# Two chained sequence blocks: casts of square sums to another engine, one recurrence to another engine, and four numbers of the schedule

## Chip, cores and metric

The kernel runs on one core of one Trainium2 chip. The metric is device time in microseconds; three runs of a kernel are summed up by their median. One more execution is profiled, and everything read from a trace below comes from that one.

## What is computed

The input is a sequence of 2048 tokens of width 1024. Two blocks follow each other.

```python
# first block: state-space mixer and short convolution
proj = rmsnorm(x) @ w_in                 # u_ssm, z_ssm, h, b, c, z (512 wide each)
s[t] = ab * s[t-1] + bb * u_ssm[t]       # complex state, 32 groups of 64 states
y = gelu(Re(c . s) + d * u_ssm)
y_ssm = y * sigmoid(y @ w_glu + b_glu) * silu(z_ssm)
y_conv = b * conv3(c * h) * silu(z)
x = rmsnorm(x + [y_ssm, y_conv] @ w_out)
# second block: conv module, gated recurrence, chunked attention, FFN
sh1, sc1, g1, sh2, sc2, g2 = silu(c_2) @ w_ada + b_ada     # modulation rows
p = (x * (1 + sc1) + sh1) @ w_in_2
y = [conv_module(p), hgrn2(p), chunk_attention(p)] @ w_out_2
x = layer_norm(ALPHA * x + (1 + g1) * y)
h = x * (1 + sc2) + sh2
x = layer_norm(ALPHA * x + (1 + g2) * ((silu(h @ W_gate) * (h @ W_up)) @ w_ffn_out))
```

## The kernel before

Every large product is made of three float16 matmuls per block (`mm3`, L417 to L419): each operand is cut into a high and a low float16 half (`split`: the high half on ScalarE, L405, the low half on VectorE, L406). The cut needs a power-of-two scale of the whole tensor, which comes from its sum of squares: ScalarE squares and adds along the free axis (`sumsq`, L410), giving one float32 number for each of 128 partitions; `part` casts these to bfloat16 (L365, or L367 where two columns are added on the way), and `total` adds over the partitions with one matmul against a matrix of ones (L373); VectorE then makes the scale from the exponent (`pow2`, L354 to L356). So a cut waits for a load, then ScalarE, the cast, TensorE, VectorE, and then the two halves of the cut. Since TensorE works in the order in which its instructions stand, a `total` whose cast is late holds up all matmuls behind it.

`Weight` and `Loader` do this for weights in three steps (load, `stat`, `split`), with `d1` and `d2` as the distances between the steps counted in weights. `Pair` and `Feed` are the same for the FFN's input weights (`load`, `scale`, `cut`, numbered 0, 1, 2); `prime` runs the first `PRIME_N` of a list of such steps in the last stage before the FFN, and `FIRST` says which are run within the FFN's first products.

The order of the program is that of a list: the stages are Python loops over column blocks and blocks of 512 tokens, and `bg.tick()` in these loops advances background generators by a rate for each. The state-space work (`ssm_all`, four feature blocks `ssm_fb`), the modulation rows (`mod_rows`, twelve rows, L768 to L777) and the loads are such generators. A scheduler then puts the instructions of each engine into their order, so a small edit shifts orders far away from it.

Within `ssm_fb`, two chains of eight complex products (`cmul`, six element-wise instructions each of 128x64) make the matrices E and H. Both run on GpSimd (`gtt`, L360). H is copied into a zero-filled matrix by ScalarE (L647, L648); L821 is ScalarE's copy of a finished projection out of PSUM.

The stage after that (`stage_glu_mix`) projects z (L1002, SiLU), applies GELU to the recurrence's output (L945), multiplies by w_glu (sigmoid, L967), and multiplies by w_out for 16 tiles of 128 tokens (L1079 adds a half tile, L1048 scales a tile, L406 cuts it). Meanwhile `ConvAtt.prep` takes nine of the second block's weights through a `Loader`.

Of the kernel before, what the change touches and what calls it, by code (L numbers as in the profile page):

```python
# [11 lines left out]
BF16 = mybir.dt.bfloat16  # L12
# [3 lines left out]
ALU = mybir.AluOpType  # L16
AX = mybir.AxisListType
# [135 lines left out]
class Weight:  # L153
# [17 lines left out]
    def stat(self):  # L171
        k = self.k
        nc = k.nc
        n = len(self.raw)
        self.pair = k.pair([P, self.nkb, self.ncol], "w")
        ss = k.tiny("wss", n)
        for c, raw in enumerate(self.raw):
            if self.colmul is not None:
                cm = self.colmul[:, c * P:(c + 1) * P].unsqueeze(1).to_broadcast([P, self.nkb, P])
                k.gtt(raw, raw, cm, ALU.mult)  # L180
            if self.rowmul is not None:
                self.mul(raw, raw, self.rowmul.unsqueeze(2).to_broadcast([P, self.nkb, P]), ALU.mult)
            k.sumsq(self.pair[1][:, :, c * P:(c + 1) * P].bitcast(BF16), raw, out=ss[:, c:c + 1])
        if n > 1:
            t = k.tiny("wst")
            nc.vector.tensor_reduce(t, ss, axis=AX.X, op=ALU.add)
            ss = t
        self.cols = k.cols3.pop(0) if len(k.cols3) > 8 else k.hold(3)
        self.tot, self.s, self.inv = (self.cols[:, i:i + 1] for i in range(3))
        self.x = k.part(self.tot, ss)  # L190

    def split(self):
        k = self.k
# [77 lines left out]
class Kit:  # L271
# [87 lines left out]
    def gtt(self, out, x, y, op):  # L359
        self.nc.gpsimd.tensor_tensor(out, x, y, op)  # L360

    def part(self, col, a, b=None):
        x = col.bitcast(BF16)[:, :1]
        if b is None:
            self.nc.vector.tensor_copy(x, a)  # L365
        else:
            self.nc.vector.tensor_tensor(x, a, b, ALU.add)  # L367
        return x

    def total(self, x, out, tot=None):  # L370
        nc = self.nc
        ps = self.bank()
        nc.tensor.matmul(ps[:, :1], self.ones, x, start=True, stop=True)  # L373
        sq = ps[:, :1]
        if tot is not None:
            nc.vector.tensor_copy(tot, sq)
            sq = tot
        self.pow2(sq, out=out)
        self.unbank(ps)
# [174 lines left out]
def ssm_fb(k, a, pm, fb, u_d, y_d):  # L554
    nc = k.nc
    gp = nc.gpsimd
    v = nc.vector
    NP = 4
    prs = slice(fb * 4, fb * 4 + 4)
    shp = [P, NP, 16]  # L560
# [17 lines left out]
    Hr, Hi = new([P, NP, 8, 16], "Hr"), new([P, NP, 8, 16], "Hi")  # L578
    t1, t2 = new(shp, "cm1"), new(shp, "cm2")

    def cmul(orr, oi, xr, xi, yr, yi):
        k.gtt(t1, xi, yi, ALU.mult)
        k.gtt(orr, xr, yr, ALU.mult)
        k.gtt(orr, orr, t1, ALU.subtract)
        k.gtt(t2, xi, yr, ALU.mult)
        k.gtt(oi, xr, yi, ALU.mult)
        k.gtt(oi, oi, t2, ALU.add)

    cmul(Er[:, :, 0], Ei[:, :, 0], br, bi, bc("qr"), bc("qi"))
    k.free(br, bi)  # L590
    for j in range(7):
        cmul(Er[:, :, j + 1], Ei[:, :, j + 1], Er[:, :, j], Ei[:, :, j], bc("abr"), bc("abi"))
        if j == 3:
            yield
    yield
    C = []
    Cb = []
    for nm, c2 in zip(("ssm_c_re", "ssm_c_im"), cs2):
# [13 lines left out]
        C.append(c)  # L612
        Cb.append(cb)
    yield
    cmul(Hr[:, :, 0], Hi[:, :, 0], C[0], C[1], bc("abr"), bc("abi"))
    k.free(*C)
    for j in range(7):
        cmul(Hr[:, :, j + 1], Hi[:, :, j + 1], Hr[:, :, j], Hi[:, :, j], bc("abr"), bc("abi"))
        if j == 3:
            yield  # L620
    k.free(t1, t2)
# [159 lines left out]
def stage_in(k, a, dr):  # L781
# [95 lines left out]
    cw = k.new([P, 4, 3], F32, "cw")  # L877
    for j in range(3):
        nc.sync.dma_start(cw[:, :, j], a["conv_w"][0, j].rearrange("(f p) -> p f", p=P))
    mod = k.bg.add(mod_rows(k, a, dr["mod"]), 0.8)  # L880
    cols = [c + fb * P for fb in range(4) for c in (2048, 1024, 1536, 2560)] + [512 + f * P for f in range(4)]
    chunks = Loader([Weight(k, win[:, c:c + P], inv_x, rowmul=gain) for c in cols])
    at = 0
# [39 lines left out]
def stage_glu_mix(k, a, xT, chunks, ssm, mod, dr, nxt):  # L923
# [50 lines left out]
    def mp1(tb):  # L974
        cv = k.new([P, 4, TB], F32, "cv")
        nc.sync.dma_start(cv, dr["yv"][:, tb * TB:(tb + 1) * TB].rearrange("(k p) t -> p k t", p=P))
        gy = G[tb][0]
        pr = k.pair([P, KB, TB], "mp")
        s2 = k.tiny("ms", 2)
        k.sumsq(pr[1][:, 0:4].bitcast(BF16), gy, out=s2[:, 0:1])  # L980
        k.sumsq(pr[1][:, 4:8].bitcast(BF16), cv, out=s2[:, 1:2])
        s, inv = k.hold(), k.hold()
        k.part(inv, s2[:, 0:1], s2[:, 1:2])
        M[tb] = [gy, cv, pr, s, inv]

    def mp2(tb):
        gy, cv, pr, s, inv = M[tb]
        k.total(inv.bitcast(BF16)[:, :1], (s, inv))
        k.split(pr[0][:, 0:4], pr[1][:, 0:4], gy, s)
        k.split(pr[0][:, 4:8], pr[1][:, 4:8], cv, s)  # L990
        k.free(gy, cv)
        sc = k.hold(2)
        for n in range(2):
            v.tensor_tensor(sc[:, n:n + 1], inv, wo[n].get(0).inv, ALU.mult)
        M[tb] = (pr, sc)
# [150 lines left out]
class ConvAtt:  # L1146
# [8 lines left out]
    def prep(self, inv_h, hb2):  # L1155
        k, a = self.k, self.a
        nc, v = k.nc, k.nc.vector
        W2 = a["w_in_2"][0]
        W = lambda c0, n=P: Weight(k, W2[:, c0:c0 + n], inv_h, bound=c0 >= 2560)
        self.ws = Loader([W(256), W(384), W(0), W(128), W(2560), W(2816), W(2688), W(2944), W(3072, 256)])  # L1160
        yield from self.ws.run()
        w = self.ws.ws
        self.wg, self.wv, self.wq, self.wk, self.wvv = w[0:2], w[2:4], w[4:8:2], w[5:8:2], w[8]

        def bscale(w):
            q = k.tiny("bq")
            v.tensor_tensor(q, w.tot, hb2, ALU.mult)
            s, i = k.pow2(q, keep=True)
            e = k.hold()
            v.tensor_tensor(e, s, w.inv, ALU.mult)  # L1170
            return s, i, e

        self.sq = [bscale(x) for x in self.wq]
        self.sk = [bscale(x) for x in self.wk]
        self.sv = bscale(self.wvv)
        qks = []
        self.qki = []
        for f in range(2):
            t = k.hold()
            v.tensor_tensor(t, self.sq[f][0], self.sk[f][0], ALU.mult)  # L1180
            qks.append(t)
            t = k.hold()
            v.tensor_tensor(t, self.sq[f][1], self.sk[f][1], ALU.mult)
            v.tensor_scalar(t, t, 0.125, None, op0=ALU.mult)
            self.qki.append(t)
        yield
        self.B = yield from att_bias(k, a, self.dr["ext"], qks)
        self.cw = k.new([P, 2, self.KC], F32, "cw")
        self.cb = k.hold(2)
        for f in range(2):  # L1190
# [686 lines left out]
class Pair:  # L1877
# [8 lines left out]

    def scale(self):
        k = self.k
        ss = k.tiny("wss", 3)
        junk = k.new([P, 4, 2 * P], BF16, "junk")  # L1890
        for i in range(2):
            k.sumsq(junk, self.raw[i], out=ss[:, i:i + 1])
        k.free(junk)
        self.inv = k.hold()
        self.x = k.part(self.inv, ss[:, 0:1], ss[:, 1:2])

    def cut(self):
        k = self.k
# [377 lines left out]
EARLY_RATE = 0  # L2276
AHEAD = 1
PRIME_AT = 11
PRIME_N = 8
SSM_RATE = 1.0  # L2280


@with_exitstack
# [71 lines left out]
```

## Time and profile before

| | us |
|---|---|
| median of three runs (lowest, highest) | 3271.31 (3270.45, 3274.15) |
| profiled execution, its own time | 3276.22 |
| its span, first to last instruction | 3274.5 |
| TensorE busy | 3048.2 |
| VectorE busy | 2061.5 |
| ScalarE busy | 1116.8 |
| GpSimd busy | 760.0 |

Of the profiled execution's time, 1.7 us lie outside the span, and it is 4.9 us above the median of the three runs. TensorE is idle for 226.3 us of the span (3274.5 - 3048.2). The granted TensorE clock, averaged over the span, is 0.967 of full speed.

### The profile page before, as it was taken

The numbers are of one execution on the slowest core, as the hardware profiler recorded it, in microseconds if no ns is written. First come the engines' busy times: TensorE is split into PE (matmuls) and PEld (weight loads), VectorE is DVE, ScalarE is ACT, GpSimd is POOL, SyncE is SP. The second block draws the span as 40 slices with busy tenths as digits, with TensorE's granted clock in tenths as the row PEclk, the third lists the DMA queues.
The fourth block names the chain that finished last, engine by engine and source line by source line (L and its number), as shares of the span: only waits on it lengthen the run. The fifth ranks groups of instructions, "written<-read, shape, count | busy, mean of one in ns | idle before, by whom it ended". The sixth has DMA issues, their size and how long they took to land. (4 is left out here: it accounts for less than half of the span.)

```text
span 3274.5 us, 43302 instructions
## 1 busy us (share of the span) xinstructions
PE 3048.2 (93%) x16198; PEld 1532.2 (47%) x16198; DVE 2061.5 (63%) x4895; ACT 1116.8 (34%) x1745; POOL 760.0 (23%) x801
## 2 busy tenths in 40 slices
PE   6799999979799988999999878999999999899998
PEld 4344454534345654555555433444444444344443
DVE  5577887355864469999568877555555555543322
ACT  5322222584524565221333333444443333300000
POOL 0432533023332332110120223111111121023321
PEclk9899999989899998999999989999999999999999
DMA  8734443535773754100125798222331113723220
GB/s 181 166 92 111 121 125 80 120 100 152 215 219 74 138 117 106 39 14 33 62 78 140 170 250 216 90 78 78 102 110 54 58 52 119 244 68 113 68 73 31
DMA packets 549651, 364.57 MB, mean 111 GB/s; under 512 B 290152, under 2 KB 503592, under 8 KB 545344
## 3 DMA queue, kind: packets, MB, share of 16 engines
q1 hardware_dynamic: 549440, 361.81, 41.1%
q8 instruction: 127, 2.08, 0.3%
q14 instruction: 84, 0.69, 0.1%
HBM read 216.73 MB, written 84.70 MB: 92 GB/s over the span
## 5 line engine op out<-in xcount | busy, mean ns | idle before, releaser
L417 PE MATMUL psum<-arena 128*128 128x512 f16 (+2 forms) x4272 | 1601.9, 377 | 78.6 <-DMA arena<-arena 34.4
L418 PE MATMUL psum<-arena 128*128 128x512 f16 (+2 forms) x4272 | 1602.1, 376 | 8.2 <-DMA arena<-h_d 4.2
L419 PE MATMUL psum<-arena 128*128 128x512 f16 (+2 forms) x4272 | 1598.6, 376 | 0.2 <-DVE arena L406 0.2
L360 POOL TENSOR_TENSOR arena<-arena 128x64 f32<-128x64 f32 (+5 forms) x681 | 681.8, 1025 | 2089.2 <-DVE arena L2179 336.9
L417 PEld LDWEIGHTS <-arena 128*128 128x128 f16 x4272 | 426.0, 100 | 593.1 <-issue 101.1
L418 PEld LDWEIGHTS <-arena 128*128 128x128 f16 x4272 | 424.1, 99 | 492.1 <-issue 44.3
L419 PEld LDWEIGHTS <-arena 128*128 128x128 f16 x4272 | 424.2, 99 | 488.4 <-issue 26.1
L410 ACT ACTIVATE arena<-arena 128x1024 bf16<-128x1024 f32 (+2 forms) x218 | 237.7, 1091 | 487.0 <-DVE arena L2062 153.3
L406 DVE SCALAR_TENSOR_TENSOR arena<-arena,kept 128x1024 f16<-128x1024 f32 (+2 forms) x152 | 230.4, 1538 | 130.0 <-ACT arena L405 110.4
L2005 DVE TENSOR_TENSOR arena<-arena,psum 128x512 f32<-128x512 f32 x264 | 177.8, 684 | 206.0 <-PE psum L419 150.9
L405 ACT ACTIVATE arena<-arena,kept 128x1024 f16<-128x1024 f32 (+2 forms) x152 | 174.5, 1175 | 183.0 <-DVE kept L355 62.7
L406 DVE SCALAR_TENSOR_TENSOR arena<-arena,ring 128x1024 f16<-128x1024 f32 (+1 forms) x164 | 209.7, 1302 | 42.0 <-ACT arena L405 36.2
L405 ACT ACTIVATE arena<-arena,ring 128x1024 f16<-128x1024 f32 (+1 forms) x164 | 172.2, 1082 | 168.6 <-DVE ring L355 100.4
L1369 DVE SCALAR_TENSOR_TENSOR arena<-arena 128x512 f32<-128x512 f32 x240 | 177.9, 778 | 0.3
L1551 PE MATMUL psum<-arena 128*127 128x64 f32 (+6 forms) x896 | 106.2, 264 | 22.2 <-DVE arena L1554 21.1
L1551 PEld LDWEIGHTS psum<-arena 128*127 128x127 f32 (+6 forms) x896 | 102.0, 182 | 48.4 <-DVE arena L1554 29.8
L2179 DVE SCALAR_TENSOR_TENSOR arena<-psum,kept,arena 128x512 f32<-128x512 f32 x32 | 23.3, 747 | 144.0 <-PE psum L419 144.0
L770 DVE SCALAR_TENSOR_TENSOR arena<-arena 128x128 f32<-128x128 f32 x336 | 111.6, 367 | 1.8
L2051 ACT ACTIVATE arena<-arena,kept 128x1024 f32<-128x1024 f32 x44 | 49.8, 1142 | 124.1 <-DVE arena L2005 124.1
L1289 ACT ACTIVATE arena<-arena,ring,kept 128x640 f32<-128x640 f32 (+4 forms) x64 | 54.5, 851 | 81.8 <-DVE ring L1287 73.0
L373 PE MATMUL psum<-kept,ones 128*128 128x1 bf16 x82 | 13.3, 169 | 70.4 <-DVE kept L365 49.5
L1553 DVE TENSOR_TENSOR arena<-arena 128x256 f32<-128x256 f32 x112 | 54.9, 490 | 37.4 <-PE psum L1551 35.8
(318 smaller groups left out, 2583.2 us busy)
## 6 DMA issues: line engine op xcount, KB each, us to landing
arena<-in_w_in_dram SPq DMA_DIRECT2D x50, 512.0 KB
arena<-in_w_ada_dram SPq DMA_DIRECT2D x48, 512.0 KB
arena<-in_w_ffn_in_dram SPq DMA_DIRECT2D x44, 512.0 KB
arena<-in_w_ffn_out_dram SPq DMA_DIRECT2D x44, 512.0 KB
a_d<-arena SPq DMA_DIRECT2D x88, 256.0 KB
arena<-a_d SPq DMA_DIRECT2D x40, 512.0 KB
arena<-in_x_dram SPq DMA_DIRECT2D x32, 512.0 KB
x_d<-arena SPq DMA_DIRECT2D x32, 512.0 KB
```

The source lines that it names most:

```text
L360: self.nc.gpsimd.tensor_tensor(out, x, y, op)
L405: self.nc.scalar.activation(hi, src, AF.Identity, scale=s)
L406: self.nc.vector.scalar_tensor_tensor(lo, src, s, hi, op0=ALU.mult, op1=ALU.subtract)
L410: self.nc.scalar.activation(junk, src, AF.Square, accum_out=ss)
L417: self.nc.tensor.matmul(ps, lh, rh, start=start and i == 0, stop=False)
L418: self.nc.tensor.matmul(ps, lh, rl, start=False, stop=False)
L419: self.nc.tensor.matmul(ps, ll, rh, start=False, stop=stop and i == n - 1)
L770: v.scalar_tensor_tensor(ac, raw[:, kb], cc[:, kb:kb + 1], ac, op0=ALU.mult, op1=ALU.add)
L1369: v.scalar_tensor_tensor(acc[:, f], src, w, acc[:, f], op0=ALU.mult, op1=ALU.add)
L1551: nc.tensor.matmul(pv[:rows, bsl], KS[:, c * P:c * P + rows], q4[:, bsl], start=True, stop=True)
L1553: v.tensor_tensor(q4, q4, Fv[:, :, 0:1].to_broadcast([P, nb, hb]), ALU.mult)
L2005: v.tensor_tensor(out, x, ps, op)
```

## The change

It has five parts. (1) `part` casts on ScalarE instead of VectorE and keeps several columns apart; `total` adds them up by one matmul for each column, so that the reduction and additions on VectorE (L186, L367) go. (2) The H chain of the first feature block runs on VectorE; its two scratch tiles are freed after E and taken anew. (3) The background rates become 0.65 (before 0.8) for the modulation rows and 1.15 (before 1.0) for the state-space work. (4) `ConvAtt.prep`'s loader has d2=3, so a weight is cut three weights after its load and not two. (5) `PRIME_N` is 6, not 8: the load and the scale of the FFN's third weight pair, (0, 2) and (1, 2), move into the FFN, where `FIRST` already names them.

```diff
+        self.x = k.part(self.cols[:, 0:2], ss)          # Weight.stat; L186's reduction is gone
-    def part(self, col, a, b=None):
-        x = col.bitcast(BF16)[:, :1]
-        if b is None:
-            self.nc.vector.tensor_copy(x, a)
-        else:
-            self.nc.vector.tensor_tensor(x, a, b, ALU.add)
+    def part(self, col, a):
+        x = col.bitcast(BF16)[:, :a.shape[1]]
+        self.nc.scalar.copy(x, a)
         return x
...
-        nc.tensor.matmul(ps[:, :1], self.ones, x, start=True, stop=True)
+        n = x.shape[1]
+        for i in range(n):
+            nc.tensor.matmul(ps[:, :1], self.ones, x[:, i:i + 1], start=i == 0, stop=i == n - 1)
...
+    ht = v.tensor_tensor if fb == 0 else k.gtt
+    if fb == 0:
+        t1, t2 = new(shp, "cm1"), new(shp, "cm2")
-        cmul(Hr[:, :, j + 1], Hi[:, :, j + 1], Hr[:, :, j], Hi[:, :, j], bc("abr"), bc("abi"))
+        cmul(Hr[:, :, j + 1], Hi[:, :, j + 1], Hr[:, :, j], Hi[:, :, j], bc("abr"), bc("abi"), ht)
...
-    mod = k.bg.add(mod_rows(k, a, dr["mod"]), 0.8)
+    mod = k.bg.add(mod_rows(k, a, dr["mod"]), 0.65)
-        self.ws = Loader([W(256), W(384), W(0), W(128), W(2560), W(2816), W(2688), W(2944), W(3072, 256)])
+        self.ws = Loader([W(256), W(384), W(0), W(128), W(2560), W(2816), W(2688), W(2944), W(3072, 256)], d2=3)
-        self.x = k.part(self.inv, ss[:, 0:1], ss[:, 1:2])
+        self.x = k.part(self.inv, ss)                   # Pair.scale
-PRIME_N = 8
-SSM_RATE = 1.0
+PRIME_N = 6
+SSM_RATE = 1.15
```

What the scheduler makes of it is shown at three places, all of them on ScalarE. Lines shift: what is L405 (cut) and L410 (square sum) before is L400 and L405 after, and L360 is the new cast.

The first place is the first feature block of the state-space work; L609/L610 (L606/L607 after) copy the inputs of H, L647/L648 copy H itself, L690 and L691 are a sine with its table load. Before:

```order
L610 ACTIVATE arena<-psum 64x4x16
L690 ACT_TABLE_LOAD
L690 ACTIVATE arena<-arena 128x257
L691 ACTIVATE arena<-arena 128x257
L647 COPY arena<-arena 64x4x128
L648 COPY arena<-arena 64x4x128
L647 COPY arena<-arena 64x4x128
L821 ACTIVATE arena<-psum,kept 128x8x64
```

And after:

```order
L607 ACTIVATE arena<-psum 64x4x16
L821 ACTIVATE arena<-psum,kept 128x8x64
L647 COPY arena<-arena 64x4x128
L648 COPY arena<-arena 64x4x128
L647 COPY arena<-arena 64x4x128
L648 COPY arena<-arena 64x4x128
L690 ACT_TABLE_LOAD
L690 ACTIVATE arena<-arena 128x257
```

One more of the projection copies L821 stands ahead of the copies of H, and the sine and its table load stand behind them.

The second place is the change from GELU (L945) to sigmoid (L967) in the gated stage. Before:

```order
L945 ACT_TABLE_LOAD
L945 ACTIVATE arena<-arena 128x512
L967 ACT_TABLE_LOAD
L967 ACTIVATE arena<-psum,arena,ring 128x512
L945 ACT_TABLE_LOAD
L945 ACTIVATE arena<-arena 128x512
L967 ACT_TABLE_LOAD
L967 ACTIVATE arena<-psum,arena,ring 128x512 x2
```

And after:

```order
L400 ACTIVATE arena<-arena,kept 128x2048 x2
L945 ACT_TABLE_LOAD
L945 ACTIVATE arena<-arena 128x512 x3
L405 ACTIVATE arena,ring<-arena 128x2048
L967 ACT_TABLE_LOAD
L967 ACTIVATE arena<-psum,arena,ring 128x512 x2
L360 CAST kept<-ring 128x2
```

Before, GELU and sigmoid take turns four times, each with a table load; after, the last three GELUs stand together ahead of the first sigmoid.

The third place is the weights of `ConvAtt.prep` among the tiles of the w_out product: the rows from the x-tile's square sum on, through the cut of two 128x2048 operands. Before:

```order
L410 ACTIVATE arena,ring<-arena 128x1024
L405 ACTIVATE arena<-arena,kept 128x2048 x2
L1048 ACTIVATE arena<-arena,ring 128x1024
L405 ACTIVATE arena<-arena,kept 128x1024
L410 ACTIVATE arena,ring<-arena 128x1024 x5
```

And after:

```order
L405 ACTIVATE arena,ring<-arena 128x1024
L360 CAST kept<-ring 128x1
L405 ACTIVATE arena,ring<-arena 128x1024
L400 ACTIVATE arena<-arena,kept 128x2048 x2
L1048 ACTIVATE arena<-arena,ring 128x1024
L400 ACTIVATE arena<-arena,kept 128x1024
L405 ACTIVATE arena,ring<-arena 128x1024
L360 CAST kept<-ring 128x1
```

Before, the second prep weight's square sum is the first of the five behind the two long cuts; after, it is the first row shown, with its cast behind it, ahead of the long cuts. On TensorE each of the nine totals of this stage moves one group of 24 matmuls later against the w_out groups, so 408 matmuls, not 432, stand between the last of them and the first matmul of the attention scores (L1280).

## Rows read from the trace of the kernel before

**Rows 1.** The page's part 1: busy time, share of the span and instructions of each engine.
```profile
PE 3048.2 (93%) x16198; PEld 1532.2 (47%) x16198; DVE 2061.5 (63%) x4895; ACT 1116.8 (34%) x1745; POOL 760.0 (23%) x801
```

**Rows 2.** TensorE's waits by releaser: us in total, times, longest.
```profile
PE psum L373 <- DVE kept L365: 49.5, 9, 12.4
...
PE psum L373 <- DVE kept L367: 20.2, 3, 18.0
...
PE psum L417 <- DVE arena L775: 4.2, 1, 4.2
```

**Rows 3.** GpSimd's groups of instructions in 128 to 146 us.
```profile
L360 POOL TENSOR_TENSOR arena<-arena 128x64 f32<-128x64 f32 x48 | 15.0, 348 | 2.8 <-ACT arena L609 2.8
```

**Rows 4.** ScalarE's timeline, 128 to 149 us: start, duration, idle before.
```profile
130.59 0.22 ACT L610 ACTIVATE arena<-psum 64x64 f32<-64x64 f32 x1
...
144.82 0.62 ACT L647 COPY arena<-arena 64x512 f32<-64x512 f32 x1 [11.88 <-POOL arena L360]
```

**Rows 5.** TensorE's timeline, 134 to 148 us.
```profile
147.35 0.47 PE L628 MATMUL psum<-ident,arena 128*128 128x128 f32 x1 [12.77 <-ACT arena L821]
```

**Rows 6.** VectorE's groups by shape, whole span: count, busy, mean ns.
```profile
L1556 DVE TENSOR_TENSOR arena<-arena 128x64 f32<-128x64 f32 x16 | 7.3, 465 | 0.2
...
L717 DVE TENSOR_TENSOR arena<-arena 128x256 f32<-128x256 f32 x16 | 6.8, 428 | 0.0
...
L523 DVE TENSOR_TENSOR arena<-arena 128x16 f32<-128x16 f32 x3 | 0.5, 169 | 0.0
```

**Rows 7.** Busy us of PE, PEld, DVE, ACT, POOL by stretch; clock, DMA, GB/s.
```profile
676.00:712.00 36.00, 26.45 (x108) 11.11 (x108) 24.84 (x44) 35.76 (x33) 10.68 (x3) 0.83 0.34 117
830.00:910.00 80.00, 51.70 (x212) 21.71 (x211) 70.02 (x170) 41.24 (x52) 31.41 (x13) 0.81 0.80 240
```

**Rows 8.** ScalarE's timeline in the gated stage, 676 to 712 us.
```profile
676.00 1.99 ACT L405 ACTIVATE arena<-arena,kept 128x2048 f16<-128x2048 f32 x1
...
681.79 1.28 ACT L945 ACT_TABLE_LOAD   x1
683.09 1.10 ACT L945 ACTIVATE arena<-arena 128x512 f32<-128x512 f32 x1
...
706.17 5.78 ACT L405 ACTIVATE arena<-arena,kept 128x2048 f16<-128x2048 f32 x3
```

**Rows 9.** TensorE's timeline, 695 to 709 us.
```profile
705.85 0.16 PE L373 MATMUL psum<-kept,ones 128*128 128x1 bf16 x1 [4.48 <-DVE kept L365]
708.22 1.01 PE L417 MATMUL psum<-arena 128*128 128x512 f16 x2 [2.20 <-ACT arena L405]
```

**Rows 10.** TensorE's timeline, 829 to 905 us.
```profile
829.25 0.38 PE L419 MATMUL psum<-arena 128*128 128x512 f16 x1
829.47 0.17 PE L373 MATMUL psum<-kept,ones 128*128 128x1 bf16 x1
829.50 0.38 PE L417 MATMUL psum<-arena 128*128 128x512 f16 x1
...
891.83 0.16 PE L373 MATMUL psum<-kept,ones 128*128 128x1 bf16 x1 [10.84 <-DVE kept L365]
...
904.56 0.16 PE L373 MATMUL psum<-kept,ones 128*128 128x1 bf16 x1 [5.10 <-DVE kept L365]
```

**Rows 11.** VectorE's timeline, 836 to 848 us.
```profile
836.44 6.69 DVE L406 SCALAR_TENSOR_TENSOR arena<-arena,kept 128x2048 f16<-128x2048 f32 x2
...
847.01 0.20 DVE L365 CAST kept<-ring 128x1 bf16<-128x1 f32 x2
```

**Rows 12.** SyncE's issues, 1934 to 1946 us.
```profile
1944.96 0.77 SPq L1885 DMA_DIRECT2D arena<-in_w_ffn_in_dram  x1
```

**Rows 13.** ScalarE's timeline, 1945 to 1955 us.
```profile
1951.38 1.06 ACT L410 ACTIVATE arena<-arena 128x1024 bf16<-128x1024 f32 x1 [10.39 <-DMA arena<-in_w_ffn_in_dram]
```

**Rows 14.** SyncE's issues, 2025 to 2030 us.
```profile
2025.15 4.05 SPq L1857 DMA_DIRECT2D arena<-h_d  x6
```

**Rows 15.** TensorE's timeline, 2050 to 2051 us, the matmul of pair 2's total.
```profile
2050.59 0.17 PE L373 MATMUL psum<-kept,ones 128*128 128x1 bf16 x1
```

More of the change, by code (lines that the diff above doesn't have):

```diff
@@ L183, in stat @@
             k.sumsq(self.pair[1][:, :, c * P:(c + 1) * P].bitcast(BF16), raw, out=ss[:, c:c + 1])
[L184 to L187, printed above, removed]
         self.cols = k.cols3.pop(0) if len(k.cols3) > 8 else k.hold(3)
         self.tot, self.s, self.inv = (self.cols[:, i:i + 1] for i in range(3))
-        self.x = k.part(self.tot, ss)
+        self.x = k.part(self.cols[:, 0:2], ss)
     def split(self):
@@ L579, in ssm_fb, with cmul @@
     t1, t2 = new(shp, "cm1"), new(shp, "cm2")
[L581 to L587, printed above, removed]
+    def cmul(orr, oi, xr, xi, yr, yi, tt=k.gtt):
+        tt(t1, xi, yi, ALU.mult)
+        tt(orr, xr, yr, ALU.mult)
+        tt(orr, orr, t1, ALU.subtract)
+        tt(t2, xi, yr, ALU.mult)
+        tt(oi, xr, yi, ALU.mult)
+        tt(oi, oi, t2, ALU.add)
     cmul(Er[:, :, 0], Ei[:, :, 0], br, bi, bc("qr"), bc("qi"))
@@ L595, in ssm_fb @@
     yield
+    if fb == 0:
+        k.free(t1, t2)
     C = []
@@ L614, in ssm_fb @@
     yield
-    cmul(Hr[:, :, 0], Hi[:, :, 0], C[0], C[1], bc("abr"), bc("abi"))
+    ht = v.tensor_tensor if fb == 0 else k.gtt
+    if fb == 0:
+        t1, t2 = new(shp, "cm1"), new(shp, "cm2")
+    cmul(Hr[:, :, 0], Hi[:, :, 0], C[0], C[1], bc("abr"), bc("abi"), ht)
     k.free(*C)
     for j in range(7):
-        cmul(Hr[:, :, j + 1], Hi[:, :, j + 1], Hr[:, :, j], Hi[:, :, j], bc("abr"), bc("abi"))
+        cmul(Hr[:, :, j + 1], Hi[:, :, j + 1], Hr[:, :, j], Hi[:, :, j], bc("abr"), bc("abi"), ht)
         if j == 3:
@@ L982, in mp1 @@
         s, inv = k.hold(), k.hold()
-        k.part(inv, s2[:, 0:1], s2[:, 1:2])
+        k.part(inv, s2)
         M[tb] = [gy, cv, pr, s, inv]
@@ L987, in mp2 @@
         gy, cv, pr, s, inv = M[tb]
-        k.total(inv.bitcast(BF16)[:, :1], (s, inv))
+        k.total(inv.bitcast(BF16)[:, :2], (s, inv))
         k.split(pr[0][:, 0:4], pr[1][:, 0:4], gy, s)
@@ L1888, in scale @@
         k = self.k
-        ss = k.tiny("wss", 3)
+        ss = k.tiny("wss", 2)
         junk = k.new([P, 4, 2 * P], BF16, "junk")
```

## Prediction

> **What bounds the kernel now.** I read first the busy times [rows 1]: TensorE works for 3048.2 of the span's 3274.5 us, so the kernel is bounded by TensorE, and only the 226.3 us in which it stands can be won, plus what it loses at a lower clock. The second view is the list of TensorE's waits [rows 2]. The largest entry is the partition total L373 waiting nine times, 49.5 us together, for the cast L365 on VectorE; L373 behind the adding cast L367 has 20.2 us more, of which 18.0 is one wait. The third is the timeline around each long gap, to see whether the cast itself is late or what comes ahead of it. Four places matter.
>
> At 134.6 to 147.35 TensorE stands 12.77 us [rows 5]. Its releaser is ScalarE's copy L821, but ScalarE had been standing 11.88 us before L647, until GpSimd ended the H chain [rows 4]: 48 instructions of 348 ns, 15.0 us [rows 3].
>
> In 676 to 712 ScalarE is busy 35.76 of 36 us [rows 7], so there the queue of ScalarE is the bound. TensorE pays with 4.48 us before a total and 2.20 us before a product [rows 9], and runs at a mean granted clock of 0.83.
>
> In 830 to 910 TensorE waits for totals of the prep weights: the longest wait of [rows 2], 12.4, then 10.84 and 5.10 [rows 10], 28.3 us. The first of these ends with a cast at 847.01, which stood on VectorE behind two cuts of 6.69 us together [rows 11]. The granted clock is at 0.81 on average here, and VectorE is busy 70.02 of 80 us [rows 7]: it is nearly the bound itself.
>
> At 1954 a total of the first FFN pair waits 18.0 us [rows 2]. The cast is not its cause: the second half of the weight was issued only at 1944.96 [rows 12], and its square sum, which ScalarE had awaited 10.39 us, began at 1951.38 [rows 13].
>
> **Part by part.** *H on VectorE.* The trace has no such chain there. The nearest rows for float32 products of two operands are 169 ns for 16 columns and 428 ns for 256 [rows 6]; in between, 64 columns give 169 + 48/240 x 259 = 221 ns, and 48 of them 10.6 us. Begun at 130.8 (after L610, [rows 4]) the chain ends at 141.4, 3.4 us before L647 began. One more L821 now stands ahead of L647 on ScalarE, which frees a PSUM bank sooner, and a table load behind it; I add 1.5 us, about a table load [rows 8] and a small copy [rows 4]. Term: -5. The upper bound is the row of 465 ns for the very shape [rows 6]: 22.3 us, 153.1, +8 us; the lower takes most of the gap, -9. I take the first since the 465 ns row lies so far above that of four times the columns that it must hold waits. What is queued behind the chain on VectorE are modulation rows and scales, a few us late at worst.
>
> *The gated stage.* Parts 1 and 3 change ScalarE's order. From 676.00 to 706.17 [rows 8] its 30.2 us hold two long cuts, three long square sums, four GELUs, eight sigmoids and eight table loads; after, the same stretch (from the two cuts to the three cuts) holds two table loads, three GELUs, two square sums and two casts. Six loads of 1.28, a GELU of 1.10 and a long square sum, taken at the long cut's 1.99, fewer, less two casts at the 0.22 of a small copy [rows 4], are 10.3 us. What was taken out stands earlier, where ScalarE has some slack, so the cut that TensorE waited for at 708.22 comes up to 10 us sooner, and both waits go: 6.7 us, and some 2 us for running at full clock behind them. Term: -9; bounds -12 (the earlier stall shrinks too) and +2 (the GELUs moved ahead lengthen that one as much).
>
> On one point page and row differ. A table load takes 1.28 us from 681.79, and the GELU behind it begins at 683.09, 0.02 us later [rows 8]. The Trainium skill, "ScalarE: Activation LUTs", section "What ACT_TABLE_LOAD costs", gives some 1.28 us for the load and a drain of some 1.38 us on top, 2.66 us for each switch. By it six switches would be 16 us and the gain in ScalarE's time 18.6; the trace shows no drain at these switches, and as TensorE's two waits are only 6.7 us the term would hardly be larger.
>
> *The prep weights.* d2=3 puts each total one group of 24 matmuls later. A matmul takes 0.22 us (829.25 to 829.47, [rows 10]), a group 5.2 us. Each of the three waits has that much more cover, and after the last total there is a group less to do. The second weight's sum and cast now stand ahead of the long cuts, so the wait of 12.4 should go. But VectorE has only 10.0 us free in this stretch; if it is the bound, TensorE merely comes earlier to the next wait. So I take the 5.2 us of the group and 3 of VectorE's slack: -8. Bounds: 0 and -18 (all slack and the group, and the lower clock regained).
>
> *More matmuls.* 45 more total matmuls at 0.03 us (829.47 to 829.50, the next one begins [rows 10]): +1.4. Most lie in the FFN, where nothing hides them.
>
> *Rates.* The modulation rows' wait of 4.2 us [rows 2] may go or appear elsewhere: 0, bounds -4 and +4. The state-space work ends sooner, which I count only through ScalarE's order above.
>
> *Prefetch.* The loads of pair 0, whose late issue makes the wait of 18.0, remain, behind about as many transposes on SyncE's queue: 0, bounds -18 and +6. Pair 2's loads move behind the loads of the FFN's input, issued until 2029.2 [rows 14]. From issue to square sum the first pair's half took 6.4 us (1944.96 to 1951.38), so pair 2's two sums can begin near 2036 and, 2.1 us of work later, the total has its input by some 2040; TensorE comes to it at 2050.59 [rows 15]. The cover is 10 us: 0. If the queue is full it costs up to +8.
>
> **Sum.** -5 - 9 - 8 + 1.4 = -20.6. From the profiled execution's own 3276.2 this gives 3255.6. That execution is 4.9 us above the median of the three runs, 3271.3, so against the median the forecast is 3251.
>
> **Rivals.** (a) *VectorE is the bound, and the gains in the w_out stretch and before it are given back.* Its 70 of 80 us speak for it; that TensorE runs without waits from 910 on, with VectorE's work postponed, against it. Then -8 becomes 0 and half the gated term is lost: -20.6 + 8 + 4.5 = -8.1, 3263. (b) *The load of pair 0 comes earlier.* SyncE's order there did change, and each step of its queue counts; against it, the loads still wait for memory that TensorE frees. Gain of up to 18 more: 3233. (c) *No gain in sum.* The lists of all engines are new from 1000 to 2036 too, where TensorE's many waits of about 2 us lie, and what is won at the four places is lost there: 3271. (d) *Slower: ScalarE's queue delays the totals.* Casts now stand in order behind cuts and square sums. Place: 676 to 910, with nine prep totals and some eight others. Price: a cast behind three long cuts is 5.78 us late [rows 8], so 17 totals could lose 98 us; it decides once the loss is over 27 us (20.6 and 0.2% of the time), that is 1.6 us for each. Against it: each cast stands directly behind its own square sum, or one instruction later. I price it at 34 us, two a total: 3285. The Trainium skill, "ScalarE: Activation LUTs", section "Rules for kernel authors", speaks for this rival, since it gives plain arithmetic to VectorE and not to ScalarE; no row here has a 128x1 copy on ScalarE.
>
> **Chances and range.** The forecast has 0.44 (its own range 3241 to 3262), (a) 0.17, (b) 0.14, (c) 0.13, (d) 0.12. A measurement of this kernel tells about 0.2%, 6.5 us, from no change. Faster are the forecast, (b), and about three quarters of (a); the same, (c) and the rest of (a), less what strays below: 0.72 faster, 0.15 the same, 0.13 slower. The range leaves out the far part of (b) and of (d): 3230 to 3279.
>
> **What would show it.** H: VectorE in place of GpSimd until about 141.4, and TensorE's gap near 8 us. Gated stage: two table loads between the pair of long cuts and the three, and no wait at 701 to 708. Prep: the three waits at or under 20 us together, none for the second weight. FFN: no wait at pair 2's total. Wrong would be waits of L373 for ScalarE's cast with long cuts ahead of it, new gaps between 1000 and 2036, or a gap at pair 0 that is gone.

## The result: slower by 0.6%

| | before | after |
|---|---|---|
| median of five runs, us | 3270.45 | 3292.38 |
| lowest to highest | 3262.63 to 3274.15 | 3281.14 to 3294.07 |
| ratio after / before, 95% interval | | 1.0063 [1.0046, 1.0081] |
| profiled execution, span | 3274.5 | 3292.4 |
| mean granted clock | 0.967 | 0.963 |

The forecast was 3251 in a range of 3230 to 3279; the time lies above both. (Of the runs below, one execution of e8 took 4424.6 us at a granted clock of 0.67, the slow state, and is left out of its row.) Page part 1 of the changed kernel, which answers to [rows 1]:

```profile
PE 3062.1 (93%) x16243; PEld 1545.2 (47%) x16243; DVE 2075.3 (63%) x4854; ACT 1118.5 (34%) x1819; POOL 737.0 (22%) x753
```

TensorE's idle time is 230.3 us (3292.4 - 3062.1), 4.0 more than before, and its busy time 13.9 us more for only 45 more instructions of 0.03 us: most of the rest goes with the lower clock (242.6 us at the lower of its two levels, before 217.4). The idle time is a balance of stops won and stops lost. Where the loss arises is read from milestones, the start of the same instruction in both traces:

| first instruction of | before, us | after, us | difference |
|---|---|---|---|
| L696 (state-space work, TensorE) | 182.3 | 175.3 | -7.0 |
| L1079 (w_out, VectorE) | 735.3 | 731.3 | -3.9 |
| L1280 (attention scores, TensorE) | 990.3 | 981.6 | -8.7 |
| L1551 (recurrence, TensorE) | 1302.7 | 1308.9 | +6.2 |
| L2005 (first FFN tile, VectorE) | 2014.5 | 2030.4 | +15.9 |
| end of TensorE | 3264.5 | 3282.3 | +17.8 |

Up to the attention the change is ahead. From there to the FFN it loses 24.6 us (15.9 + 8.7). TensorE's timeline at the places of the prediction (start, duration, in brackets the idle time before):

```profile
141.30 0.41 PE L637 MATMUL psum<-arena 128*128 128x32 f32 x2 [3.70 <-DVE ring L350]
...
675.76 1.87 PE L412 MATMUL psum<-arena 128*128 128x512 f16 x4 [13.84 <-ACT arena L400]
...
704.33 1.86 PE L412 MATMUL psum<-arena 128*128 128x512 f16 x4 [4.95 <-ACT arena L400]
...
887.54 0.16 PE L368 MATMUL psum<-kept,ones 128*128 128x1 bf16 x1 [4.48 <-ACT kept L360]
...
901.34 0.19 PE L368 MATMUL psum<-kept,ones 128*128 128x1 bf16 x2 [6.00 <-ACT kept L360]
...
1967.62 0.19 PE L368 MATMUL psum<-kept,ones 128*128 128x1 bf16 x2 [8.29 <-DVE ring L383]
...
1996.18 0.19 PE L368 MATMUL psum<-kept,ones 128*128 128x1 bf16 x2 [5.93 <-DVE arena L401]
...
2065.60 0.19 PE L368 MATMUL psum<-kept,ones 128*128 128x1 bf16 x2
...
2819.65 0.16 PE L368 MATMUL psum<-kept,ones 128*128 128x1 bf16 x1 [6.96 <-ACT kept L360]
```

L412 to L414 are the products and L368 the total (L417 to L419 and L373 before), L400/L401 the cut, L405 the square sum, L360 the new cast. The gap of [rows 5] is 3.70 us and not 12.77. The total waits of [rows 10] are two, 10.5 us, where there were three of 28.3. Pair 0 waits 8.29 instead of 18.0 [rows 2], pair 1 5.93 instead of 1.90, and pair 2, at 2065.60, does not wait, as in [rows 15]. Busy time by stretch (columns as in [rows 7]) in the changed kernel, the two stretches of [rows 7] first, then first score matmul to first recurrence matmul, and the second half of the recurrence:

```profile
676.00:712.00 36.00, 30.99 (x127) 12.73 (x126) 24.16 (x42) 26.72 (x28) 16.19 (x3) 0.84 0.29 103
830.00:910.00 80.00, 59.17 (x236) 24.76 (x235) 67.52 (x148) 41.52 (x57) 32.13 (x12) 0.85 0.84 237
981.60:1308.90 327.30, 282.42 (x2506) 173.34 (x2505) 197.06 (x595) 179.56 (x312) 100.16 (x97) 0.91 0.52 107
1596.30:1853.20 256.90, 237.89 (x1363) 143.47 (x1361) 185.32 (x520) 79.70 (x180) 34.15 (x18) 0.95 0.34 98
```

And the last two of these stretches in the kernel before:

```profile
990.30:1302.70 312.40, 278.63 (x2495) 169.76 (x2494) 197.71 (x598) 177.10 (x300) 92.38 (x77) 0.94 0.55 114
...
1583.10:1831.70 248.60, 234.25 (x1361) 139.59 (x1359) 180.16 (x522) 75.81 (x173) 33.90 (x18) 0.97 0.35 99
```

With nearly the same number of instructions on each engine but GpSimd (97, before 77) the attention takes 14.9 us longer (327.3 - 312.4), at a clock of 0.91, not 0.94. The other engines are little fuller for it: VectorE's and ScalarE's sums differ by -0.7 and +2.5 us, GpSimd's by 7.8 of 327.3 us. TensorE stands 11.1 us more there (44.9, before 33.8) and is busy 3.8 us more; in the second half of the recurrence it stands 4.7 us more and is busy 3.6 more. Those two stretches lose 23.2 us; the first half of the recurrence loses 7.0 more, and the last stage ahead of the FFN wins 5.6. One spot of the attention, TensorE's timeline in 1206 to 1223 us after the change, and its busy time in 1213 to 1238:

```profile
1213.30 0.20 PE L1321 MATMUL psum<-arena 128*128 128x64 f16 x1 [3.27 <-DMA arena<-arena]
...
1217.79 0.21 PE L1323 MATMUL psum<-arena 128*128 128x64 f16 x1 [1.92 <-DMA arena<-arena]
...
1222.04 0.59 PE L412 MATMUL psum<-arena 128*128 128x512 f16 x1 [3.39 <-DMA arena<-h_d]
```

```profile
1213.00:1238.00 25.00, 14.57 (x93) 7.97 (x94) 15.26 (x27) 17.66 (x29) 8.19 (x6) 0.52 0.81 185
```

Three waits for transfers end within 9 us, six smaller ones, 4.7 us together, come between and behind them until 1231.8, and the granted clock is at its lower level (0.52 on average) for these 25 us. The kernel before has such small waits too, in other places. That the whole loss is made of such spots is not shown wait by wait; the idle time above is its greater part.

### The profile page after: what moved, and what is told of

It is laid out like the page before. It is cut to its first block, busy times and chain, and to the rows that moved or that the text cites. A ratio compares the mean times of both kernels' runs of the same rounds, so it can differ in the third digit from the quotient of the medians.

```text
span 3292.4 us, 43400 instructions
## 1 busy us (share of the span) xinstructions
PE 3062.1 (93%) x16243; PEld 1545.2 (47%) x16243; DVE 2075.3 (63%) x4854; ACT 1118.5 (34%) x1819; POOL 737.0 (22%) x753
## 5 line engine op out<-in xcount | busy, mean ns | idle before, releaser
L412 PE MATMUL psum<-arena 128*128 128x512 f16 (+2 forms) x4272 | 1605.4, 377 | 78.8 <-ACT arena L400 31.2
L414 PE MATMUL psum<-arena 128*128 128x512 f16 (+2 forms) x4272 | 1600.8, 376 | 10.0 <-DMA arena<-arena 10.0
L356 POOL TENSOR_TENSOR arena<-arena 128x64 f32<-128x64 f32 (+4 forms) x633 | 656.7, 1060 | 2071.8 <-DVE arena L2179 338.5
L412 PEld LDWEIGHTS <-arena 128*128 128x128 f16 x4272 | 426.9, 100 | 549.9 <-issue 89.5
L414 PEld LDWEIGHTS <-arena 128*128 128x128 f16 x4272 | 424.6, 99 | 501.3 <-issue 29.4
L405 ACT ACTIVATE arena<-arena 128x1024 bf16<-128x1024 f32 (+1 forms) x218 | 238.1, 1092 | 528.2 <-DVE arena L2062 212.2
L2005 DVE TENSOR_TENSOR arena<-arena,psum 128x512 f32<-128x512 f32 x264 | 177.4, 684 | 241.7 <-PE psum L414 166.5
L401 DVE SCALAR_TENSOR_TENSOR arena<-arena,kept 128x1024 f16<-128x1024 f32 (+2 forms) x152 | 223.7, 1495 | 108.8 <-ACT arena L400 94.1
L400 ACT ACTIVATE arena<-arena,kept 128x1024 f16<-128x1024 f32 (+2 forms) x152 | 174.3, 1176 | 197.7 <-DVE kept L351 62.6
L400 ACT ACTIVATE arena<-arena,ring 128x1024 f16<-128x1024 f32 (+1 forms) x164 | 169.8, 1083 | 155.2 <-DVE ring L351 96.0
L401 DVE SCALAR_TENSOR_TENSOR arena<-arena,ring 128x1024 f16<-128x1024 f32 (+1 forms) x164 | 205.6, 1297 | 20.9 <-ACT arena L400 20.4
L1551 PE MATMUL psum<-arena 128*127 128x64 f32 (+6 forms) x896 | 110.3, 270 | 29.6 <-DVE arena L1554 27.7
L1551 PEld LDWEIGHTS psum<-arena 128*127 128x127 f32 (+6 forms) x896 | 106.3, 188 | 56.0 <-DVE arena L1554 36.9
L770 DVE SCALAR_TENSOR_TENSOR arena<-arena 128x128 f32<-128x128 f32 x336 | 118.4, 384 | 1.7
L1553 DVE TENSOR_TENSOR arena<-arena 128x256 f32<-128x256 f32 x112 | 59.3, 530 | 29.3 <-PE psum L1551 28.6
L356 POOL TENSOR_TENSOR arena<-arena,kept 128x1024 f32<-128x1024 f32 x21 | 45.2, 2152 | 133.1 <-DMA arena<-in_w_in_dram 83.6
```

The source lines that it names most:

```text
L400: self.nc.scalar.activation(hi, src, AF.Identity, scale=s)
L401: self.nc.vector.scalar_tensor_tensor(lo, src, s, hi, op0=ALU.mult, op1=ALU.subtract)
L405: self.nc.scalar.activation(junk, src, AF.Square, accum_out=ss)
L412: self.nc.tensor.matmul(ps, lh, rh, start=start and i == 0, stop=False)
L414: self.nc.tensor.matmul(ps, ll, rh, start=False, stop=stop and i == n - 1)
L770: v.scalar_tensor_tensor(ac, raw[:, kb], cc[:, kb:kb + 1], ac, op0=ALU.mult, op1=ALU.add)
```

## The experiments

Theories: **A**, the loss is that of another order of instructions in attention and recurrence, in which the parts of the change only have the role of a push; **B**, ScalarE's queue holds casts and cuts back (rival (d)); **C**, the parts themselves cost what they do in their own stages, or the addresses of buffers do. Ratios are to the kernel before, with 95% intervals.

| run | what it has | median, us | ratio |
|---|---|---|---|
| e1 | part 1 (casts) | 3270.18 | 1.0009 [0.9998, 1.0021] |
| e7 | part 2 (H), scratch tiles kept | 3263.15 | 0.9990 [0.9976, 1.0003] |
| e2 | part 3 (rates) | 3294.15 | 1.0071 [1.0056, 1.0086] |
| e3 | part 4 (d2) | 3281.55 | 1.0038 [1.0024, 1.0053] |
| e4 | part 5 (six steps) | 3266.07 | 0.9986 [0.9975, 0.9996] |
| e8 | all but part 3 | 3278.79 | 1.0029 [1.0016, 1.0043] |
| e5 | none, loader held | 3291.91 | 1.0076 [1.0059, 1.0094] |
| e6 | part 3, loader held | 3274.66 | 1.0023 [1.0012, 1.0035] |
| e10 | all five, loader held | 3267.12 | 0.9998 [0.9988, 1.0008] |
| e9 | none, other addresses | 3266.32 | 0.9992 [0.9979, 1.0004] |
| e11 | parts 2 and 5 | 3258.45 | 0.9975 [0.9963, 0.9987] |
| e12 | parts 1, 2 and 5 | 3260.29 | 0.9985 [0.9975, 0.9996] |

**One part each.** The edits are the lines of the diff above, each alone, for example

```diff
-SSM_RATE = 1.0
+SSM_RATE = 1.15                 # with 0.65 for mod_rows: e2
-PRIME_N = 8
+PRIME_N = 6                     # e4
```

e1: 

> Before with part 1 alone: casts on ScalarE, one total matmul per column. Theory A (the loss is the new order of instructions in the second block's attention and recurrence, 1000 to 1750 us, brought by the parts that move background work: rates, d2 and memory): this kernel is within 0.2% of before, 3264 to 3278 us, and the stretch from the first score matmul to the last recurrence matmul (840 us before) is within 5 us of it. Theory B (ScalarE's queue holds casts and cuts back, wherever it is busy): slower by 10 to 20 us, 3281 to 3291, with TensorE's waits for ScalarE's cuts above the 18.8 us of before and waits for ScalarE's cast of 20 us or more. Both: the FFN's last total waits some 3 us longer than before.

e2: 

> Before with part 3 alone: 0.65 for the modulation rows and 1.15 for the state-space work. Theory A: the second block's attention and recurrence take 10 to 30 us longer, the time is 3275 to 3295. Theory B: no loss, 3260 to 3275, since no cast moved. Both: the state-space work ends some 45 us sooner.

e3: 

> Before with part 4 alone: d2=3 in the loader of the nine prep weights. From the prediction: the three waits of 28.3 us at 834 to 905 shrink to 20 us or less, the stretch gains 5 to 8 us. Theory A: part of that, or all, is lost again from 1000 to 1750 us, time 3265 to 3290. Theory B: the gain stays, 3260 to 3267.

e4: 

> Before with part 5 alone: PRIME_N = 6. Nothing ahead of the last stage of the second block changes, so both theories say the time to 1850 us stays within 2 us. Prediction's term: 0, 3271; the wait of 18.0 at the first pair's total may shrink, as it did to 8.3 us in the changed kernel: then 3260 to 3266. No wait of TensorE at the third pair's total in either case.

As the cause of the loss B falls with e1: all casts stand on ScalarE, and the time is the same. TensorE's waits from 820 to 925 in e1, and the first two of them in its timeline:

```profile
PE psum L368 <- ACT kept L360: 28.3, 4, 9.0
```

```profile
845.36 0.16 PE L368 MATMUL psum<-kept,ones 128*128 128x1 bf16 x1 [8.96 <-ACT kept L360]
...
873.99 0.16 PE L368 MATMUL psum<-kept,ones 128*128 128x1 bf16 x1 [5.19 <-ACT kept L360]
```

The sum is that of before's three waits, but the four waits are not the same ones. ScalarE's timeline before, the end of the square sum behind the longest wait:

```profile
843.02 0.19 ACT L410 ACTIVATION_READ_ACCUMULATOR arena<-arena 128x1 f32 x1
```

It ended at 843.21, after the two cuts of [rows 11] (843.13), behind which the prediction saw the cast; the cast came only at 847.01, kept 3.8 us by a third cut and other work on VectorE. In e1 the cast begins at 845.11, right behind its square sum (until 845.08), and the wait is 8.96, not 12.4. The wait at 873.99 is new: its square sum ended at 870.7, and the cast came 3.0 us later, at 873.76, behind a tile's scale and two cuts on ScalarE. This is the mechanism of rival (d). So the cast was late once on either engine; ahead of the other waits it came within 1 us of its square sum, and there the square sum was what came late. That both sums are 28.3 is chance.

The rates alone bring the whole loss, 0.71%. The work that they move ends long before the attention (in e2 the state-space work at 567.3 us, before 615.9, and the modulation rows at 654.0, before 566.5), and the first score matmul of e2 comes at 988.9, before at 990.3: all that e2 loses, it loses behind. d2 alone costs 0.38%, although d2 is 6.3 us ahead at the first score matmul (984.0, before 990.3): it has lost that by the first recurrence matmul and more behind it. Part 5 alone gains some 4 us, where the sum had 0. It is not the wait of pair 0 (19.05 us in e4, before 18.0), as the expectation had it; its place is the start of the FFN, TensorE's waits in 2005 to 2070 before:

```profile
PE psum L417 <- DVE arena L2005: 3.0, 3, 1.0
PE psum L418 <- DMA arena<-h_d: 1.6, 1, 1.6
PE psum L417 <- ACT arena L2010: 1.3, 1, 1.3
PE psum L417 <- DMA arena<-h_d: 0.8, 1, 0.8
```

and the only one there in e4:

```profile
PE psum L417 <- DVE arena L2005: 1.0, 1, 1.0
```

**The same push without the change.** e5 takes the kernel before and lets the loader of the recurrence's weights stop after three weights until the projections of the last block of tokens (`ca.proj`) are written; e6 is part 3 with the same lines:

```diff
-            if nxt.k.sb.room() - nxt.ncol * nxt.nkb * 2 >= reserve:
+            held = reserve and self.n[0] >= 3 and not getattr(nxt.k, "go", False)
+            if not held and nxt.k.sb.room() - nxt.ncol * nxt.nkb * 2 >= reserve:
...
+            k.go = True
```

e5: 

> Before with none of the five parts. One line holds the recurrence's weight loader back from its fourth weight until the last h tile of the attention stage has been asked for; as the emitted order shows, this takes away the two background steps that before makes while it waits there for memory, and the third recurrence head of the second token block starts one step later, as in the kernels with the rates or with d2=3. Theory A, made sharper (the loss is the emitted order of the recurrence stage, which follows from when a buffer finds room in the arena): slower by 0.3 to 0.7%, 3280 to 3293, all of it after the first score matmul at 990 us. Theory C (the rates lose time by what they do in the first block, or by the addresses of buffers): within 0.15% of before.

e6: 

> Part 3 alone (the rates) with the same line as in the kernel before this one. The two then emit the recurrence stage in nearly the same order. Theory A: within 5 us of that kernel, and less than the 3294 of the rates alone if that order is the better one. Theory C: 3290 to 3297, as with the rates alone.

Without any part of the change the kernel is as slow as the changed one, and with the rates in this other order the loss of the rates shrinks from 0.71% to 0.23%. A's forecast that both would be within 5 us of each other missed by 12: this line does not fix the order alone (the table below has two different ones). In e5 the attention waits elsewhere. The longest of TensorE's groups in 990 to 1310 us:

```profile
PE psum L1281 <- DVE ring L1285: 10.7, 5, 7.1
```

In the kernel before the same wait, L1280 for L1284, has 3.6 us in five times, the longest 1.5. Yet the attention of e5 is only 2.1 us longer than before. The second half of its recurrence and the last stage ahead of the FFN lose the rest:

```profile
1583.60:1841.00 257.40, 236.40 (x1361) 144.02 (x1359) 181.49 (x521) 75.81 (x173) 34.22 (x18) 0.96 0.33 95
1841.00:2028.70 187.70, 156.32 (x697) 69.45 (x696) 157.94 (x356) 66.77 (x89) 49.58 (x35) 0.93 0.94 224
```

They have 248.6 and 182.8 us before. So e5 loses as much as the change in all, but not at the same places.

**H alone, and the change without its rates.** e7 leaves out the freeing and new taking of the two scratch tiles; e8 is the changed kernel with the rates 0.8 and 1.0.

e7: 

> Before with part 2 alone, H of the first feature block on VectorE; the scratch tiles are kept, not freed and taken anew, since the arena has no room for that in before's order. Emitted order elsewhere is that of before. Prediction's term: -5 (bounds -9 and +8): 3262 to 3268, with VectorE's chain of 48 instructions taking 10.6 us by the interpolated row, 22 by the other, and the gap of 12.8 us at 134.6 to 147.4 near 8 us. If the gain of 8.7 us that the changed kernel has at the first projections is H's, it shows here too: 6 to 9 us ahead at 182 us.

e8: 

> The changed kernel with part 3 taken back (rates as before), parts 1, 2, 4 and 5 in. If the parts add up: 3270 + 1 (casts) - 7 (H) + 12 (d2) - 4 (prefetch) = 3272. Theory A: the sum of single parts need not hold, since d2 alone already changes the emitted order of the recurrence stage; 3265 to 3290, with the difference from before at 1302 to 1832 us as the order decides. Theory B: as the changed kernel, 3285 to 3295.

VectorE's H chain in e7 has 48 instructions of 215 to 216 ns. At L696 (here L697) e7 is 3.5 us ahead (178.8, before 182.3), not 6 to 9. The single parts add up to +2.9 - 3.3 + 23.2 + 12.4 - 4.6 = +30.6 us (ratios by 3268), the whole change has +20.6 (0.63%): they are not additive, and leaving out the part that costs 23 alone gives back only 11.

**Addresses, the whole change in another order, and the parts that don't push.** e9 only takes a buffer that nothing needs and sets it to zero; e10 is the changed kernel with e5's lines; e11 and e12 combine lines shown above.

```diff
+    pad = k.sb.new([P, 8], F32, "pad")      # e9
```

e9: 

> The kernel before with one more buffer of 8 float32 columns taken first and kept, so that every later buffer lies elsewhere in the arena; no part of the change, and the instructions come out in the same coarse order as before (the recurrence's weights are loaded at the same places among the attention's steps). Theory A (the loss comes from another order of attention and recurrence): within 6 us of before, since this order is kept. Theory C (addresses or how neighbours in memory reuse each other's room matter by themselves): some 10 us or more to either side, with the milestones moving between 1000 and 1850.

e10: 

> All five parts of the change, and the line that holds the recurrence's loader, which alone cost 24 us. It puts the recurrence's weights at yet another place of the program. Theory A: the milestones up to the first score matmul stay as in the changed kernel (some 9 us ahead of before), and from there to the FFN the loss is another number than +26 us, anywhere from -10 to +40, which the parts cannot tell. If the parts themselves slow the kernel (what ScalarE, VectorE and the rates do in the stages themselves), the loss stays within 5 us of the changed kernel's: 3292 plus the 20 that the line costs alone, or 3292.

e11: 

> Parts 2 and 5 alone (H on VectorE with its scratch tiles kept, six prefetch steps): the two parts that by themselves lost nothing and that leave the order of the recurrence's loads as before. Theory A: the two gains add up, -6 to -10 us, 3259 to 3264 where before is 3269. If gains ahead of the attention are given back there whatever the order is (rival c), only the -4 us of part 5 stay.

e12: 

> Parts 1, 2 and 5: as the run with parts 2 and 5, and all casts on ScalarE. The order of the recurrence's loads is again that of before. Theory A: no loss in the attention, 3258 to 3268, below the kernel before. Theory B (the casts on ScalarE hold totals and cuts back once the other parts have moved work on ScalarE): 3275 or more, with the extra time between 660 and 910.

Theory A could not say e10's sign, only that it would not be the changed kernel's time. e10 decides against C: the same lines that cost the kernel before 0.76% take from the changed one all that it lost, with every part still in it. Up to the first score matmul e10 runs as the changed kernel does (981.4 and 981.6, before 990.3). The stretches behind it in e10, first score to first recurrence matmul and the second half of the recurrence:

```profile
981.40:1296.30 314.90, 280.91 (x2505) 172.03 (x2504) 206.17 (x605) 177.93 (x312) 101.56 (x97) 0.93 0.54 113
...
1580.30:1826.30 246.00, 230.69 (x1362) 139.92 (x1363) 181.31 (x520) 75.17 (x174) 32.30 (x17) 0.98 0.37 103
```

314.9 and 246.0 us, where the changed kernel has 327.3 and 256.9. e9 leaves the order as it was and stays within the interval of no change, so this shift of addresses alone does not bring the loss. e11 and e12 keep the order of before and lose nothing in the attention, as A expected; e11 has the lowest median and beats both kernels, and the casts that e12 adds bring nothing more. No run has part 3 or part 4 in the order of before, since each of them brings another.

Whether the order is kept can be read off a trace: how many score matmuls (L1280) stand ahead of the second to fourth totals behind the first score matmul, and how many recurrence matmuls (L1551) ahead of the two totals that stand among them. Beside it the time from the first score matmul to the first FFN tile, L2005:

| kernel | score matmuls | recurrence matmuls | us |
|---|---|---|---|
| before | 245, 275, 275 | 664, 776 | 1024.2 |
| e1, e4, e7, e9, e11, e12 | 245, 275, 275 | 664, 776 | 1021.4, 1018.0, 1016.8, 1016.6, 1015.7, 1005.0 |
| e10 (all, held) | 235, 255, 265 | 624, 672 | 1019.2 |
| e6 (rates, held) | 230, 241, 245 | 624, 672 | 1021.3 |
| e8 (without rates) | 220, 230, 235 | 664, 776 | 1025.0 |
| e3 (d2) | 230, 235, 255 | 624, 672 | 1031.0 |
| e5 (none, held) | 230, 250, 250 | 624, 776 | 1040.1 |
| e2 (rates) | 210, 220, 230 | 624, 776 | 1042.7 |
| after | 230, 244, 254 | 624, 672 | 1048.8 |

The six that keep the order of before need 1005 to 1021 us and before itself 1024, the seven others 1019 to 1049; in medians of the whole, the six have 3258 to 3270, the seven 3267 to 3294. (The profiled execution of before, 3276.2, is 5.8 us above the median of its five runs, so differences of profiled milestones make other kernels look a few us too good.) Which step of the order costs how much is not settled by these runs: e10 and the changed kernel have nearly the same counts and lie 30 us apart. The counts tell that an order is another one, not what it costs.

## Why the prediction was wrong, step by step

**Wrong step: rates "0, bounds -4 and +4", and with it the price of rival (c).** The prediction counted part 3 by the wait of 4.2 us that it might move and by ScalarE's order in one stage. By the code, the rates move what lies in memory when the recurrence's weights ask for room, and `Loader.run` puts a step off while there is none; that the list of the attention and the recurrence comes out in another order, the counts of e2 show. Measured alone: +23 us (e2). Part 4 has the same gap in its term: the prep weights were priced in their own stage alone, and d2 alone costs 12 us (e3). Rival (c) named the place rightly, 1000 to 2036, but took the loss there as just what is won elsewhere; it was 24.6 us in the trace against 8.7 won. Its own sentence, that the lists of all engines are new there, should have had a price with both signs: the seven other orders run here lie from 5 us below to 25 above the kernel before from the first score matmul to the FFN, and 8.4 above it on average (a mean of 1032.6, less 1024.2). Among the orders run here that of before was a good one for this stretch, and a change of it an exposure.

**Wrong step: the gated stage, "-9".** The time moved by +3.1 (from -7.0 to -3.9). The arithmetic on ScalarE held; that the waits go with it did not. TensorE's stall ahead of the two long cuts, before:

```profile
678.04 1.87 PE L417 MATMUL psum<-arena 128*128 128x512 f16 x4 [10.54 <-ACT arena L405]
```

ScalarE's timeline between the two and the three long cuts, after:

```profile
673.72 3.88 ACT L400 ACTIVATE arena<-arena,kept 128x2048 f16<-128x2048 f32 x2
...
684.77 1.91 ACT L405 ACTIVATE arena<-arena 128x2048 bf16<-128x2048 f32 x1 [2.78 <-POOL arena L356]
...
694.47 1.91 ACT L405 ACTIVATE arena<-arena 128x2048 bf16<-128x2048 f32 x1 [3.51 <-DVE arena L969]
...
702.28 5.79 ACT L400 ACTIVATE arena<-arena,kept 128x2048 f16<-128x2048 f32 x3 [2.16 <-DVE kept L351]
```

From 673.72 to 702.28 are 28.6 us, 9.2 of them idle (2.78 + 3.51 + 2.16 and 0.77 behind a total): 19.3 us of work, 10.8 less than the 30.2 of [rows 8] (forecast 10.3 less). But the square sums now wait for GpSimd's and VectorE's products and the cuts for a scale from VectorE, so the three cuts begin only 1.6 us sooner behind the two. The wait of 4.48 before a total [rows 9] went; the wait of 2.20 at 708.22 [rows 9] became 4.95, and the stall ahead, which stood as a bound in the prediction (the GELUs moved ahead lengthen it), grew from 10.54 to 13.84. From 640 to 712 TensorE waits 18.8 us in all, before 18.0, and the granted clock in [rows 7]'s first stretch is 0.84, before 0.83, so the 2 us for a full clock, which no row had, did not come either. The queue of ScalarE was full in that stretch, and still it was not the only thing that TensorE waited for.

**Right, but the credit was small: H, "-5".** The trace has -7.0 at L696, the gap 3.70 us and not 8. The 221 ns for one instruction were nearly right (215 to 216 in e7), but 48 of them are not 10.6 us, since each begins before the one ahead has ended. VectorE's timeline in e7, first and last instruction of the chain, and what follows:

```profile
131.11 0.23 DVE L583 TENSOR_TENSOR arena<-arena 128x64 f32<-128x64 f32 x1 [0.22 <-ACT arena L609]
...
138.17 0.21 DVE L587 TENSOR_TENSOR arena<-arena 128x64 f32<-128x64 f32 x1
...
141.56 2.18 DVE L771 SCALAR_TENSOR_TENSOR arena<-arena 128x128 f32<-128x128 f32 x8
143.66 0.21 DVE L354 TENSOR_SCALAR ring<-psum 128x1 int32<-128x1 int32 x2
```

The chain takes 7.3 us (131.11 to 138.38), one instruction each 0.135 us where nothing stands between. [rows 3] has the same in small: 48 times 348 ns would be 16.7 us, not 15.0. In the changed kernel it takes 10.3 us (127.44 to 137.75), with one instruction of 2.74 us in it (below). And still TensorE stands 8.77 us in e7, until 143.87:

```profile
143.87 0.64 PE L638 MATMUL psum<-arena 128*128 128x32 f32 x2 [8.77 <-DVE ring L354]
```

It now waits for a scale on VectorE, L354, which stands behind modulation rows (L771). These are the rows that the prediction saw queued behind the chain, "a few us late at worst", and left out of its sum. In this kernel, with the order unchanged, the whole part is worth some 3 us, and its interval reaches no change.

**Right in direction: the prep weights, "-8".** The time moved by -4.8 (from -3.9 to -8.7). Total waits shrank from 28.3 to 10.5, but three waits for VectorE's L1079 came up: rival (a), in half. TensorE's waits from 820 to 925, after:

```profile
PE psum L368 <- ACT kept L360: 10.5, 2, 6.0
PE psum L412 <- DVE arena L1079: 10.3, 3, 4.2
```

VectorE is busy 67.52 of 80 us there, TensorE 59.17 instead of 51.70.

**Right: the extra totals,** 0.03 us each: the second matmul of a pair's total at 2065.63 follows the first at 2065.60. **Prefetch, "0":** pair 2 has no wait, as said; part 5 gains 4 us (e4) by small waits at the start of the FFN, which the prediction did not look at. Parts 1 to 4 without part 5 were not run.

**A place that was missed: FFN's last block.** On ScalarE's queue, after,

```profile
2817.32 1.06 ACT L405 ACTIVATE arena<-arena 128x1024 bf16<-128x1024 f32 x1 [1.67 <-DVE ring L351]
...
2818.38 1.13 ACT L400 ACTIVATE arena<-arena,ring 128x1024 f16<-128x1024 f32 x1
2819.42 0.18 ACT L360 CAST kept<-ring 128x1 bf16<-128x1 f32 x1
2819.50 3.22 ACT L400 ACTIVATE arena<-arena,ring 128x1024 f16<-128x1024 f32 x3
```

the cast stands behind a cut of 1.13 us, as in rival (d), and the total before which TensorE waited 4.02 us waits 6.96. But the cut is not the reason: from the end of the square sum to the total are 1.17 us, before 0.95, and e1 has the same order of these instructions, where the total waits 4.13 us and not the 3 us more that were expected. In the changed kernel the square sum itself comes late, having waited 1.67 us for VectorE's L351 (a wait of 0.23 us in e1); e12 waits 5.65 us, which is not followed here.

## What to carry to other kernels

Where buffers and background steps decide the order in which a program is written, a small number such as a rate or a distance is an edit to every later stage: compare the lists far behind the edit first, and give an unlooked-for order a price with both signs. Test a slow version by pushing the order in another way (hold one load, take one pad buffer): if the time moves as much as by the change, the change's own merits are still unmeasured. And a chain's length is read from the starts of its instructions, not from their mean duration times their number. Then keep the parts that leave the order alone, here H on VectorE and six prefetch steps, 0.25% faster than before.

## What the runs showed of the hardware

An element-wise instruction of two tensors on VectorE can stand still while GpSimd works, with nothing in the program between them. VectorE's timeline of the changed kernel,

```profile
128.99 2.74 DVE L579 TENSOR_TENSOR arena<-arena 128x64 f32<-128x64 f32 x1
...
890.32 1.68 DVE L1167 TENSOR_TENSOR ring<-kept 128x1 f32<-128x1 f32 x1
...
892.04 0.14 DVE L350 TENSOR_SCALAR ring<-ring 128x1 int32<-128x1 int32 x1
892.16 2.16 DVE L192 TENSOR_TENSOR kept<-kept 128x1 f32<-128x1 f32 x1
```

and GpSimd's:

```profile
129.75 1.90 POOL L356 TENSOR_TENSOR arena<-arena,kept 128x1024 f32<-128x1024 f32 x1
...
889.63 4.67 POOL L356 TENSOR_TENSOR arena<-arena 128x1024 f32<-128x1024 f32 x2 [8.57 <-DVE arena L1046]
```

The 128x64 instruction takes 2.74 us where those behind it take 0.21 to 0.23, and ends at 131.73, as GpSimd's at 131.65. The two of 128x1, some 0.15 us elsewhere, end at 892.00 and 894.32; GpSimd's pair ends at 894.30 (889.63 + 4.67), and half of it is past at 891.97. The instruction with one tensor input at 892.04, while GpSimd works, took 0.14. In e7 one of 128x4 takes 4.55 us and ends at 127.07, as GpSimd's pair of 128x1024 at 127.05. So a small scale on VectorE, behind which a cut and a total stand, was some 2 us late in the changed kernel, by all signs for an instruction of another engine. The Trainium skill, "GPSIMD Engine Reference", section "1. Specifications", says that GpSimd shares its SBUF interfaces with VectorE and contends with VectorE instructions that have two SBUF inputs; the trace agrees.

A cast of 128x1 takes 0.18 us on ScalarE (L360, 2819.42), and on VectorE 0.16 (before, 847.64; the 0.20 of [rows 11] are two casts). And the waits of 3.27, 1.92 and 3.39 us, with the six smaller ones, came with 23.9 us at the lower clock level in a row, from 1213.4 on, while TensorE was busy 14.57 of 25 us. Behind the wait at 704.33, matmuls of 128x512 begin 0.43 us apart (706.63, 707.06, 707.49) while the clock is at that level, and 0.22 us apart from 708.28 on, when it is at the higher: such waits can cost more than they last.
